# Sample attention with page products in bursts of 16 per four pages, six page buffers, and steps with small array tiles set next to each other

## The chip, the core and the metric

One core of a Trainium2 chip runs the whole program. The metric is the device time of one execution, in microseconds (us). The engines are TensorE (PE), VectorE (DVE), ScalarE (ACT), GpSimd (POOL) and SyncE (SP), which here issues most DMA loads. PE's array has 128 rows and 128 columns; a product may use a part of it, such as 128 rows by 32 columns, and up to four of those lie side by side.

## The reference

One decoder layer for a prompt (512 tokens and 16 meta tokens) and for 8 samples of 8 new tokens, each with 2,048 cached tokens in pages of 128. Differential attention and gated DeltaNet read the same normalised input; their outputs are gated, merged and projected, and a gated ConvFFN follows. The part that the change touches most is the attention of the samples over their cached pages:

```python
k_past = cache_k[l][page_table].reshape(ds, -1, DA_HEADS, 2, DA_HEAD_DIM)
v_past = cache_v[l][page_table].reshape(ds, -1, DA_HEADS, 2 * DA_HEAD_DIM)
...
s_past = jnp.einsum('bqhmd,bkhmd->bhmqk', qs, k_past, preferred_element_type=jnp.float32)
...
pr = jax.nn.softmax(jnp.concatenate([s_past, s_new], axis=-1), axis=-1)
a = pr[:, :, 0] - lam * pr[:, :, 1]
out = (jnp.einsum('bhqk,bkhe->bqhe', a[..., :n_past], v_past.astype(jnp.float32))
       + jnp.einsum('bhqk,bkhe->bqhe', a[..., n_past:], v.astype(jnp.float32)))
```

## The kernel before

The program is written as streams of steps (Python generators). `merge` runs several streams and picks, each time, the stream that has done the smallest share of its planned work (`e[2]` over its weight). A step ends with `yield`, and a number after it is the time, in estimated PE work, for which the stream stays back before its next step, so that ACT and DVE can finish what the next step needs. The numbers come from `DELAY`, or from `PAUSES`, a table that overrides them by stream and by the number of the step. So the order of the instructions of every engine is fixed when the program is built: the merge writes them in an order, and a scheduler then sets the final order by priority and readiness.

Two streams run side by side for the first half of the time: `main` (attention of the prompt, then DeltaNet for four heads, with `gdn_chain`, `gdn_base` and `gdn_solve`) and `rest` (attention of the samples, then the gates and a branch's projection). Behind them come the merge of the branches, the output projection and the ConvFFN, which the change leaves as they are.

`sample_attention` takes two samples at a time (`pr`, four pairs). Its first half goes over four groups `g` of four key pages per sample. For each half group `u` and each sample `e`, `pages` loads two pages (one tile "page", 128x2x512, from a pool of five), PE transposes them (8 transpositions to PSUM "ps_t", of which there are three banks), and ACT or DVE copies them to "KT" (four buffers). Then, after a pause, 8 products of "KT" with "qb" go to "ps_s". Each product uses 128 rows by 32 columns of the array, and the four heads lie side by side. The second half, after the softmax, transposes the probabilities "S" to "pT" and multiplies them with the value pages: 8 products per two tiles "page", again in 32 columns per head.

Loads go through SP's queue in the order of the program; each page load waits until its buffer is free. Products of the DeltaNet's solve use 32x32, 64x64 and other parts of the array; products with weights and the transpositions use the whole.

`qT` (the prompt's queries), `on` (a head's DeltaNet output) and `z2` (its gate) have tiles of their own.

Of the kernel before, what the change touches and what calls it, by code (L numbers as in the profile page):

```python
# [18 lines left out]
SEQ = 512  # L19
# [5 lines left out]
NPG = PAST // PAGE  # L25
H = 4
# [25 lines left out]
def _lay_out_constants():  # L52
# [67 lines left out]
    for name, a in (("c0", c0), ("c1", c1), ("m0", m0), ("m1", m1)):  # L120
# [26 lines left out]
PAUSES = {  # L147
    "gdn_chain0": {
        0: 4.0, 2: 0.87, 3: 0.3, 8: 26.28, 9: 0.49, 10: 0.23, 11: 1.4, 12: 1.21, 13: 0.66, 15: 0.56, 16: 2.98,
        18: 0.39, 19: 0.44, 20: 0.45, 21: 0.63, 22: 0.08, 23: 0.99, 25: 0.74, 26: 0.8, 27: 0.26, 29: 0.85, 33:  # L150
        2.26,
    },
    "gdn_chain1": {
        0: 2.24, 5: 0.96, 8: 25.17, 9: 0.12, 10: 0.89, 11: 0.11, 12: 0.47, 13: 0.57, 15: 1.02, 16: 1.35, 17:
        0.57, 18: 0.28, 19: 1.05, 20: 1.89, 21: 0.59, 24: 0.63, 25: 0.85, 26: 0.37, 27: 0.04, 28: 0.71, 29:
        0.97,
    },
    "gdn_chain2": {
        3: 0.29, 4: 4.82, 7: 0.13, 8: 22.2, 9: 0.02, 10: 0.98, 11: 0.13, 13: 0.08, 15: 1.9, 16: 3.25, 17: 1.24,
        18: 0.74, 19: 1.65, 20: 0.36, 21: 0.38, 22: 0.42, 23: 1.46, 24: 0.23, 25: 0.93, 26: 1.03, 28: 0.54, 29:  # L160
        1.38, 31: 0.02, 33: 0.13,
    },
    "gdn_chain3": {
        8: 19.96, 9: 1.4, 10: 0.21, 11: 1.16, 13: 0.09, 15: 1.11, 16: 2.38, 18: 0.15, 23: 0.5, 25: 0.43, 27:
        0.24, 28: 0.37, 29: 0.39, 30: 0.33,
    },
    "gdn_project0": {
        0: 0.27, 4: 0.32, 6: 4.89,
    },
    "gdn_project1": {  # L170
        2: 0.06, 3: 1.09, 4: 0.1, 6: 35.55,
    },
    "gdn_project2": {
        0: 0.13,
    },
    "main0": {
        6: 0.56, 7: 0.4, 28: 0.8, 42: 0.04, 52: 0.15, 77: 0, 83: 0.89, 86: 0.7, 125: 1.29, 177: 0.4, 192: 0.33,
        201: 0.01, 204: 1.43, 225: 0.46, 241: 1.39, 246: 1.63,
    },
    "make0": {  # L180
        5: 0.99, 6: 0.28, 13: 0.34, 16: 0.4,
    },
    "prompt_rows0": {
        1: 1.38, 3: 7.07, 4: 1.29,
    },
    "prompt_rows2": {
        0: 6.67, 1: 1.83, 4: 0.63,
    },
    "prompt_rows3": {
        2: 0.01, 3: 3.3, 4: 1.66,  # L190
    },
    "prompt_rows4": {
        1: 0.98, 3: 2.79, 4: 1.53,
    },
    "prompt_rows5": {
        2: 0.05, 4: 0.75,
    },
    "prompt_rows6": {
        3: 2.54, 4: 0.64,
    },  # L200
    "prompt_rows7": {
        1: 1.31,
    },
# [7 lines left out]
    },  # L211
    "use0": {
        0: 0.07, 12: 1.51, 13: 0.06, 25: 3.34, 38: 2.47, 39: 0.02, 51: 1.68,
    },
}
# [12 lines left out]
FINE = 8  # L228
MAIN_1 = 582.0
MAIN_2 = 1e9  # L230
REST_W = 163.1

# [2196 lines left out]
```

## Time and profile before

| | |
|---|---|
| median of 3 runs | 1120.28 us (1118.43 to 1120.84) |
| profiled execution, its own time | 1120.4 us |
| its span, first to last instruction | 1118.5 us |
| PE busy / weight loads busy | 1095.2 us / 957.6 us |
| DVE, ACT, POOL busy | 727.8, 520.9, 221.1 us |
| DMA | 156.88 MB, 140 GB/s in the mean |
| granted PE clock | 0.997 |
| key page products (ps_s<-KT,qb) | 512 records, 37.9 us busy |
| value page products (ps_s<-page,pT) | 512 records, 34.4 us busy |

A float32 product with weights that are not float32r stands in the profile as two records, so 16 records are a burst of 8 products. A row of the timeline merges records of the same kind that follow each other; its first number is the start of the first, its second the time to the end of the last, and the xN their count. Since ends overlap, the distance from one row's start to the next row's is what a row costs. Busy times of groups are unions, so four products side by side are not counted four times.

### The profile page before, as it was taken

Reading aid. Unit: us, or ns where it says so; the run is one execution under the profiler, and the core shown is the slowest. Engines: PE = TensorE matmul, PEld = TensorE weight load, DVE = VectorE, ACT = ScalarE, POOL = GpSimd, SP = SyncE. Lnnn points to the kernel's source line nnn. Section 1 sums busy time; section 2 is a strip of 40 time slices with the busy share of each in tenths; the row PEclk is TensorE's granted clock in tenths of the full one; section 3 lists DMA queues with packets and bytes.
Section 4 is the critical chain, followed back from the end, with each engine's and each line's share of the span. In section 5 each row is a group of like instructions: output and inputs, shape, how many; then the busy total and the mean of one; then the engine's idle time right before and its main releaser. Section 6 shows DMA issues by size and latency. Waiting matters only on the chain.

```text
span 1118.5 us, 23304 instructions
## 1 busy us (share of the span) xinstructions
PE 1095.2 (98%) x8554; PEld 957.6 (86%) x8554; DVE 727.8 (65%) x1893; ACT 520.9 (47%) x1256; POOL 221.1 (20%) x340
## 2 busy tenths in 40 slices
PE   9999999999999999999999999999999999999997
PEld 8887787777686697699999987999999999988886
DVE  6455665777486387385345665599999999852315
ACT  6244454555456266352433344465555555832311
POOL 3122220121110100100000004334445454200000
PEclk9999999999999999999999999999999999999999
DMA  7377325747847857833334254423333232333213
GB/s 201 74 247 225 91 71 191 229 131 238 275 149 249 295 153 238 279 83 76 77 79 141 86 162 143 119 67 88 103 87 104 86 106 76 116 113 104 86 47 123
DMA packets 167356, 156.88 MB, mean 140 GB/s; under 512 B 12307, under 2 KB 123458, under 8 KB 167241
## 3 DMA queue, kind: packets, MB, share of 16 engines
q1 hardware_dynamic: 162833, 147.00, 43.1%
q0 software_dynamic: 3008, 5.16, 1.5%
q10 hardware_dynamic: 1400, 3.22, 0.9%
q8 instruction: 68, 1.11, 0.4%
q14 instruction: 47, 0.39, 0.1%
HBM read 145.45 MB, written 9.88 MB: 139 GB/s over the span
## 4 chain that ended last, share of the span: by engine, by line
PE 85%; DMA 4%; ACT 4%; DVE 3%; issue 1%; POOL 1%; SPq 0%; DVEq 0%; ACTq 0%; POOLq 0%
PE ps_d L357 33%; PE ps_t L357 21%; PE ps_g L357 15%; PE ps_s L357 8%; PE ps_t L512 7%; DMA page<-in_cache_v 1%; ACT KT L1566 1%; PE ps_m L357 1%; DMA wraw<-in_w_out 1%; DMA x<-in_x_prompt 1%; DMA page<-in_cache_k 1%; DMA wraw<-in_w_in 1%; ACT whi L406 1%; DVE wlo L407 1%; POOL grr L476 1%
## 5 line engine op out<-in xcount | busy, mean ns | idle before, releaser
L407 DVE TENSOR_TENSOR wlo<-wraw,whi 128x512 fp32r<-128x512 f32 x190 | 143.5, 772 | 109.9 <-ACT whi L406 108.7
L357 PE MATMUL ps_d<-xhi,whi 128*128 128x256 f32 (+2 forms) x696 | 214.2, 311 | 0.1
L357 PE MATMUL ps_d<-xhi,wlo 128*128 128x256 f32 (+2 forms) x696 | 208.7, 303 | 0.0
L357 PE MATMUL ps_d<-xlo,whi 128*128 128x256 f32 (+2 forms) x696 | 208.3, 302 | 0.0
L406 ACT CAST whi<-wraw 128x512 fp32r<-128x512 f32 x190 | 114.0, 620 | 170.1 <-PE ps_d L357 67.6
L357 PEld LDWEIGHTS ps_d<-xhi,whi 128*128 128x128 f32 x696 | 131.8, 191 | 6.5 <-issue 4.3
L357 PEld LDWEIGHTS ps_d<-xlo,whi 128*128 128x128 f32 x696 | 131.5, 190 | 3.6 <-issue 3.2
L357 PEld LDWEIGHTS ps_d<-xhi,wlo 128*128 128x128 f32 x696 | 131.0, 190 | 2.6 <-issue 2.2
L407 DVE TENSOR_TENSOR lw<-sw,hw 128x512 fp32r<-128x512 f32 x76 | 68.7, 904 | 5.2 <-ACT hw L406 5.2
L1566 ACT COPY KT<-ps_t 128x512 f32<-128x512 f32 x106 | 56.7, 596 | 28.4 <-PE ps_t L512 27.9
L512 PE MATMUL ps_t<-consts,page 128*128 128x128 f32 x512 | 67.7, 278 | 1.4 <-DMA page<-in_cache_k 0.6
L357 PE MATMUL ps_t<-fhit,hw 128*128 128x290 f32 x228 | 67.9, 298 | 1.1 <-ACT p L2018 0.6
L512 PEld LDWEIGHTS ps_t<-consts,page 128*128 128x128 f32 x512 | 55.4, 140 | 14.4 <-issue 8.2
L357 PE MATMUL ps_t<-flot,hw 128*128 128x290 f32 x228 | 67.5, 296 | 0.0
L357 PE MATMUL ps_t<-fhit,lw 128*128 128x290 f32 x228 | 67.5, 296 | 0.0
L406 ACT CAST hw<-sw 128x512 fp32r<-128x512 f32 x76 | 46.9, 619 | 15.5 <-PE ps_g L357 9.9
L357 PEld LDWEIGHTS ps_t<-fhit,hw 128*128 128x128 f32 x228 | 43.0, 189 | 1.6 <-ACT p L2018 0.9
L2069 ACT ACTIVATE fy<-fpre,fw 128x592 f32<-128x592 f32 x22 | 19.5, 884 | 51.7 <-DVE fpre L2029 51.7
L357 PEld LDWEIGHTS ps_t<-flot,hw 128*128 128x128 f32 x228 | 43.2, 189 | 0.0
L357 PEld LDWEIGHTS ps_t<-fhit,lw 128*128 128x128 f32 x228 | 43.0, 189 | 0.0
L357 PE MATMUL ps_s<-KT,qb 128*32 128x256 f32 x512 | 37.9, 386 | 0.6
L357 PE MATMUL ps_s<-page,pT 128*32 128x256 f32 x512 | 34.4, 384 | 3.2 <-DMA page<-in_cache_v 3.2
(720 smaller groups left out, 2814.3 us busy)
## 6 DMA issues: line engine op xcount, KB each, us to landing
page<-in_cache_k SPq DMA_DIRECT2D x128, 256.0 KB, 4.3
page<-in_cache_v SPq DMA_DIRECT2D x128, 256.0 KB, 4.4
wraw<-in_w_in SPq DMA_DIRECT2D x86, 256.0 KB, 3.1
wraw<-in_w_ffn_in SPq DMA_DIRECT2D x50, 256.0 KB, 3.1
wraw<-in_w_down SPq DMA_DIRECT2D x44, 256.0 KB, 2.8
raw<-in_w_ffn_in SPq DMA_DIRECT2D x38, 256.0 KB, 2.9
wraw<-in_w_out SPq DMA_DIRECT2D x16, 256.0 KB, 3.1
x<-in_x_prompt SPq DMA_DIRECT2D x4, 512.0 KB, 6.8
```

What stands on the lines that cost most here:

```text
L357: return self.nc.tensor.matmul(out, lhsT, rhs, **kw).ins
L406: self.nc.scalar.copy(hi, raw)
L407: (eng or self.nc.vector).tensor_tensor(out=lo, in0=raw, in1=hi.bitcast(F32), op=ALU.subtract)
L476: nc.gpsimd.tensor_tensor(out=dst, in0=dst, in1=self.mhalf[:rows, :n], op=ALU.pow)
L512: self.nc.tensor.transpose(out, in_, self.ident[:k, :k])
L1566: copy(kt[:, :, 128 * j : 128 * j + 128], tp)
L2069: nc.scalar.activation(y, pre[:, 0:592], AF.Identity, bias=fw[:, m, 19:20], scale=fw[:, m, 16:17])
```

## The change

There are five parts.

1. In `sample_attention` the key products of both half groups are written behind the transpositions of all four tiles: 16 products in one burst per group instead of 8 twice. The value products likewise: four tiles are loaded, then 16 products. The pause between the two bursts of a value group is gone.
2. The page pool has six buffers (`PAGES`) instead of five.
3. Three tiles are no longer made: `on` uses `vn`, `z2` uses `self.ob[:, h]`, `qT` uses `self.oa`.
4. `mm` and `transpose` note whether the last product was small (`narrow`: at most 64 rows, or at most 32 columns). After a small product, `merge` first tries the streams whose next step is marked as small (`Narrow`, `Held`), and a step marked `Held` stays back up to 3.0 longer unless the last product was a small one. The first small product behind a wide one is kept in the program's order by the scheduler.
5. `PAUSES` is a new table, and three weights of the streams are new (`MAKE_W`, `MAIN_1`, `REST_W`).

```diff
-MAKE_W = 65.20437
+PAGES = 6
+MAKE_W = 54.400005891
...
-MAIN_1 = 582.0
+MAIN_1 = 564.54
+HOLD = 3.0
+PAUSES = {
+    "gdn_chain0": {
+        0: 1.49, 2: 0.41, 3: 0.46, 4: 8.2, 6: 0.03, 8: 26.44, 9: 0.34, 10: 0.77, 11: 1.4, 12: 1.21, 13: 1.01,
...
-REST_W = 163.1
+REST_W = 162.95320999999998
+class Narrow(float):
+    hold = 0.0
+class Held(Narrow):
+    hold = HOLD
...
     def mm(self, out, lhsT, rhs, **kw):
...
-        return self.nc.tensor.matmul(out, lhsT, rhs, **kw).ins
+        was, self.narrow = self.narrow, lhsT.shape[0] <= 64 or lhsT.shape[1] <= 32
+        i = self.nc.tensor.matmul(out, lhsT, rhs, **kw)
+        return (self.tc.keep_in_program_order(i) if self.narrow and not was else i).ins
...
     def merge(self, *streams):
-        live = [[g, total, 0.0, 0.0, *self.pauses(g)] for g, total in streams]
+        live = [[g, total, 0.0, 0.0, self.pauses(g), 0, None] for g, total in streams]
         while live:
-            for s in sorted(live, key=lambda e: e[2] / (e[1]() if callable(e[1]) else e[1])):
-                if s[3] > self.work + self.idle + 1e-6:
+            now = self.work + self.idle + 1e-6
+            for s in sorted(live, key=lambda e: (
+                not (self.narrow and e[6] is not None), e[2] / (e[1]() if callable(e[1]) else e[1])
+            )):
+                if s[3] > now or s[6] is not None and not self.narrow and s[3] + s[6] > now:
                     continue
...
-                    s[3] = self.work + self.idle + s[4].get(s[5], delay)
+                    s[3] = self.work + self.idle + s[4].get(s[5], float(delay))
                     s[5] += 1
+                    s[6] = getattr(delay, "hold", None)
...
-        on = self.t(pool, [128, 5, 128], "on")
+        on = vn
...
-        yield DELAY[h][7]
+        yield Narrow(DELAY[h][7])
...
-        z2 = self.t(pool, [128, NQ], "z2")
+        z2 = self.ob[:, h]
...
-        self.qT = self.t(pool, [128, H, SEQ], "qT")
+        self.qT = self.oa
...
-            t = self.t(pool, [128, 2, 512], "page", bufs=5)
+            t = self.t(pool, [128, 2, 512], "page", bufs=PAGES)
...
-                        kts.append(kt)
-                    yield DELAY[pr][26]
-                    for e, kt in reversed(list(enumerate(kts))):
+                        kts[u, e] = kt
+                    yield Held(DELAY[pr][26]) if u else 0.0
+                for u in (1, 0):
+                    for e in (1, 0):
                         for h in range(H):
...
-                yield DELAY[pr][28]
-                for j0 in (0, 2):
-                    vps = [pages(cv, [(2 * pr + e) * NPG + 4 * g + j for e in range(2)]) for j in (j0, j0 + 1)]
-                    for k in (1, 0):
+                yield Held(DELAY[pr][28])
+                vps = [pages(cv, [(2 * pr + e) * NPG + 4 * g + j for e in range(2)]) for j in range(4)]
+                for k in (3, 2, 1, 0):
...
-                    yield DELAY[pr][31]
+                yield DELAY[pr][31]
```

What this does to the order is best seen on PE. Here x4 is a count of instructions (products or transpositions), and the numbers behind names tell the buffers of one name apart.

First place: key pages of the last pair of samples, where little else stands between. Before, a burst of two rows (8 products) follows every two tiles:

```order
L357 MATMUL ps_s_6315<-KT_6393,qb_357 32x256 x4
L357 MATMUL ps_s_6315<-KT_6377,qb_357 32x256 x4
L512 MATMUL ps_t_6435<-consts_66,page_6416 128x128 x2
L512 MATMUL ps_t_6454<-consts_66,page_6441 128x128 x4
L512 MATMUL ps_t_6460<-consts_66,page_6441 128x128 x4
L512 MATMUL ps_t_6478<-consts_66,page_6474 128x128 x4
L512 MATMUL ps_t_6484<-consts_66,page_6474 128x128 x2
L357 MATMUL ps_s_6415<-KT_6453,qb_357 32x256 x4
L357 MATMUL ps_s_6415<-KT_6428,qb_357 32x256 x4
L512 MATMUL ps_t_6484<-consts_66,page_6474 128x128 x2
```

Now, on the same engine at the same place, four rows (16 products) follow four tiles:

```order
L541 MATMUL ps_t_6456<-consts_66,page_6443 128x128 x4
L541 MATMUL ps_t_6462<-consts_66,page_6443 128x128 x4
L541 MATMUL ps_t_6472<-consts_66,page_6468 128x128 x4
L541 MATMUL ps_t_6478<-consts_66,page_6468 128x128 x4
L541 MATMUL ps_t_6488<-consts_66,page_6484 128x128 x4
L541 MATMUL ps_t_6494<-consts_66,page_6484 128x128 x4
L541 MATMUL ps_t_6531<-consts_66,page_6518 128x128 x4
L541 MATMUL ps_t_6537<-consts_66,page_6518 128x128 x2
L381 MATMUL ps_s_6417<-KT_6487,qb_356 32x256 x4
L381 MATMUL ps_s_6417<-KT_6471,qb_356 32x256 x4
L381 MATMUL ps_s_6417<-KT_6455,qb_356 32x256 x4
L381 MATMUL ps_s_6417<-KT_6430,qb_356 32x256 x4
```

What moved: the two bursts of a group stand together, and the transpositions of the next group's first tile stand ahead of the burst.

Second place: value pages of the third pair, beside the DeltaNet's chain (ps_g) and a projection (ps_d). Before, on PE, a burst takes two tiles:

```order
L357 MATMUL ps_s_5401<-page_5609,pT_5569 32x256 x4
L357 MATMUL ps_s_5401<-page_5588,pT_5569 32x256 x4
L357 MATMUL ps_g_5638<-grhs_5622,y_4895 128x128
L357 MATMUL ps_d_5751<-xhi_9_87,wlo_5718 128x322
L357 MATMUL ps_d_5751<-xhi_9_87,whi_5717 128x322
L357 MATMUL ps_d_5751<-xlo_10_88,whi_5717 128x322
L357 MATMUL ps_g_5681<-gv_5640,kn_4559 128x128
```

Now it takes four, and the next burst stands 21 rows behind:

```order
L381 MATMUL ps_s_5275<-page_5602,pT_5552 32x256 x4
L381 MATMUL ps_s_5275<-page_5599,pT_5552 32x256 x4
L381 MATMUL ps_s_5275<-page_5596,pT_5552 32x256 x4
L381 MATMUL ps_s_5275<-page_5575,pT_5552 32x256 x4
L381 MATMUL ps_g_5621<-gv_5573,kn_4788 128x128
L381 MATMUL ps_g_5625<-gS_5560,er_4761 128x128
L381 MATMUL ps_g_5625<-gv_5573,dbig_up_4780 128x128
L381 MATMUL ps_d_5890<-xlo_10_88,whi_5801 128x336
```

What moved: the work that stood between two half bursts stands behind the whole one.

Third place: the solve of the last head (32x32 products from "cc", "dd") beside the last keys. Before, PE has weight products between the small ones:

```order
L357 MATMUL ps_g_6645<-cc_6308,lm_6642 32x32 x16
L357 MATMUL ps_d_7099<-xlo_8_86,whi_7092 128x256
L357 MATMUL ps_d_7099<-xhi_7_85,wlo_7093 128x256
L357 MATMUL ps_s_6515<-KT_6601,qb_357 32x256 x4
L357 MATMUL ps_s_6515<-KT_6585,qb_357 32x256 x4
L357 MATMUL ps_g_6663<-dd_6644,row_6306 32x32 x16
```

Now the small ones of both streams follow each other:

```order
L381 MATMUL ps_s_6517<-KT_6608,qb_356 32x256
L381 MATMUL ps_g_6571<-cc_6302,lm_6568 32x32 x16
L381 MATMUL ps_s_6517<-KT_6608,qb_356 32x256 x3
L381 MATMUL ps_s_6517<-KT_6592,qb_356 32x256
L381 MATMUL ps_g_6621<-dd_6570,row_6300 32x32 x16
L381 MATMUL ps_s_6517<-KT_6592,qb_356 32x256 x3
L381 MATMUL ps_s_6517<-KT_6555,qb_356 32x256
L381 MATMUL ps_g_6641<-cc_6302,dbig_low_5950 32x32 x8
```

What moved: the weight products left the stretch, and the key burst is cut into pieces by the solve's steps, in part within the four products of one tile.

More of the change, by code (lines that the diff above doesn't have):

```diff
@@ L240, in __init__ @@
         self.work = self.idle = 0.0
-        self.made = {}
+        self.made, self.narrow, self.step = {}, False, None
     def name(self, s):
@@ L367, in pauses @@
         self.made[n] = self.made.get(n, -1) + 1
[L368 removed]
+        return PAUSES.get(f"{n}{self.made[n]}", {})
     def merge(self, *streams):
[L374 removed]
+        live = [[g, total, 0.0, 0.0, self.pauses(g), 0, None] for g, total in streams]
         while live:
[L376 to L377 removed]
+            now = self.work + self.idle + 1e-6
[3 more added lines that the diff above has]
+                if s[3] > now or s[6] is not None and not self.narrow and s[3] + s[6] > now:
                     continue
                 before = self.work
+                self.step = s
                 try:
@@ L511, in transpose @@
         self.work += 0.11
-        self.nc.tensor.transpose(out, in_, self.ident[:k, :k])
+        was, self.narrow = self.narrow, k <= 64 or in_.shape[1] <= 32
+        i = self.nc.tensor.transpose(out, in_, self.ident[:k, :k])
+        return (self.tc.keep_in_program_order(i) if self.narrow and not was else i).ins
     def embed(self, pool):
@@ L1098, in gdn_chain @@
             )
-            yield DELAY[h][9]
+            yield Narrow(DELAY[h][9]) if i == 1 else DELAY[h][9]
             if i == 1:
```

144 lines of the change are left out of this document (64 added, 80 removed), and 39 rows, old and new, of the table PAUSES.

## The prediction

> **What bounds the kernel now.** I read the page's busy times and its chain first, then the stretch in which the change lies, then who TensorE (PE) waited for there.
>
> ```profile
> PE 1095.2 (98%) x8554; PEld 957.6 (86%) x8554; DVE 727.8 (65%) x1893; ACT 520.9 (47%) x1256; POOL 221.1 (20%) x340
> PE 85%; DMA 4%; ACT 4%; DVE 3%; issue 1%; POOL 1%; SPq 0%; DVEq 0%; ACTq 0%; POOLq 0%
> 60.00:475.00 415.00, 402.78 (x3838) 314.21 (x3837) 267.32 (x958) 207.61 (x578) 65.03 (x127) 1.00 0.64 204
> PE ps_s L357 <- DMA page<-in_cache_v: 3.2, 4, 1.8
> PE ps_t L512 <- DVE kn L1005: 2.3, 2, 1.4
> PE ps_t L512 <- DVE on L1511: 2.0, 2, 1.0
> ```
>
> PE is busy for 98% of the span and is 85% of the chain. In the third row, the stretch from the first page transposition to the last value page (60 to 475 us), PE is busy for 402.8 of 415 us at a granted clock of 1.00, so only 12.2 us of idle time can be won or lost by waits as they are. The next three rows are the longest of those waits. So the change is worth what it takes from, or adds to, PE's busy time, plus the new idle time. "Busy" hides something, though: the distance from one product's start to the next differs with its neighbours. That is where the change works.
>
> ```profile
> 258.32 0.66 PE L512 MATMUL ps_t<-consts,page 128*128 128x128 f32 x4
> 258.90 1.07 PE L357 MATMUL ps_s<-KT,qb 128*32 128x256 f32 x16
> 259.91 2.26 PE L512 MATMUL ps_t<-consts,page 128*128 128x128 f32 x18
> 272.58 1.93 PE L357 MATMUL ps_s<-page,pT 128*32 128x256 f32 x32
> 274.45 0.45 PE L357 MATMUL ps_g<-cc,lm 32*32 32x32 f32 x32
> 274.83 0.65 PE L512 MATMUL ps_t<-consts,S 128*128 128x128 f32 x4
> 275.42 0.45 PE L357 MATMUL ps_g<-dd,row 32*32 32x32 f32 x32
> 276.92 1.07 PE L357 MATMUL ps_s<-page,pT 128*32 128x256 f32 x16
> 277.92 0.44 PE L357 MATMUL ps_g<-dd,row 32*32 32x32 f32 x16
> 406.28 0.66 PE L512 MATMUL ps_t<-consts,page 128*128 128x128 f32 x4
> 406.69 0.36 PE L357 MATMUL ps_d<-xlo,whi 128*128 128x256 f32 x1
> 406.89 1.51 PE L512 MATMUL ps_t<-consts,page 128*128 128x128 f32 x12
> 408.16 0.37 PE L357 MATMUL ps_d<-xhi,wlo 128*128 128x256 f32 x1
> ```
>
> The first column is the start; "128*32" is the part of the array that a product uses (rows by columns), and an f32 product of pages stands as two records, so 16 records are 8 products. One burst of 16 holds PE from 258.90 to 259.91, 1.01 us. A burst of 32 holds it from 272.58 to 274.45, 1.87 us. So 16 more records cost 0.86 us and the burst itself has a fixed part of 0.15 us. The wide neighbours pay too: four transpositions between two small shapes take 274.83 to 275.42, 0.59 us, while twelve in an undisturbed row take 406.89 to 408.16, 0.106 us each, 0.42 for four. That is 0.17 more. The weight products (float32r) show the same:
>
> ```profile
> 266.31 0.39 PE L357 MATMUL ps_d<-xhi,whi 128*128 128x256 f32 x1
> 266.53 0.28 PE L357 MATMUL ps_d<-xlo,whi 128*128 128x256 f32 x1
> 266.65 0.28 PE L357 MATMUL ps_d<-xhi,wlo 128*128 128x256 f32 x1
> 267.25 0.27 PE L357 MATMUL ps_d<-xlo,whi 128*128 128x256 f32 x1
> 267.46 0.43 PE L357 MATMUL ps_s<-kTs,qb 128*32 128x64 f32 x16
> ```
>
> They start 0.12 us apart (266.53 to 266.65), but 0.22 after the first one behind a small burst and 0.21 before the next: 0.10 and 0.09 more. So one visit to a small shape from the full array costs 0.15 + 0.17 = 0.32 us, or 0.15 + 0.19 = 0.34, beyond its work; I take 0.30, since the neighbour's part is shared where a visit is followed by another.
>
> **The change part by part.** *Bursts and neighbours.* Counted through PE's whole order, the array is left for a smaller shape and entered again 129 times before and 85 times now: 44 visits fewer, 13.2 us at 0.30. The work is the same 7,400 products. Changes from one small shape straight to another rise from 24 to 42. Their price is in 276.92 to 277.92: a burst of 16 between two small groups still holds PE for 1.00 us, 0.14 over the 0.86 of its work; I take 0.15, so 18 cost 2.7 us. In two of the four heads the steps now cut groups of four column tiles in two (place three in the part on the change, rows with a product alone and then x3); each cut sends one pass more, about a quarter of 0.86, 0.2 us, and there are 14 against 8 before: 1.2 us. Net -9.3, with bounds of -6 (visits at 0.22, cuts doubled) and -14 (visits at 0.34, small-to-small at 0.1).
>
> *Key copies.* Before, each burst of 8 key products stands close behind the transpositions that feed it:
>
> ```profile
> 336.29 1.07 PE L357 MATMUL ps_s<-KT,qb 128*32 128x256 f32 x16
> 337.29 2.04 PE L512 MATMUL ps_t<-consts,page 128*128 128x128 f32 x16
> 339.38 1.07 PE L357 MATMUL ps_s<-KT,qb 128*32 128x256 f32 x16
> L1566 ACT COPY KT<-ps_t 128x512 f32<-128x512 f32 x106 | 56.7, 596 | 28.4 <-PE ps_t L512 27.9
> ```
>
> Sixteen transpositions take 337.29 to 339.38, 2.09 us, where 16 x 0.106 + 0.17 gives 1.87: some 0.1 to 0.2 us is the wait for the last copy to KT (0.596 us). With half as many bursts, about 12 of these go: -1.4 us. On the other side stands that KT still has four buffers and one burst now uses all four, so copies of the next group wait for this group's products. In the row, PE's own pace is 4 x 0.106 = 0.42 us a tile and ACT's copy 0.6 us or a little less when piped, so over the eight tiles of a group ACT falls up to 1.4 us behind, of which three PSUM banks take up most. I put both together at -0.5, between -2 and +5.
>
> *Transpositions among weight products.* Runs of either kind become shorter: changes between them rise by about 60, 30 visits. 406.28 to 408.16 holds such a visit: 16 transpositions and one product in 1.88 us, against 16 x 0.106 + 0.12 = 1.82. At up to 0.04 each, +0.5 (0 to +1.2).
>
> *Value pages.* A burst now needs four tiles (two pages each) of six buffers at once; before it needed two of five. All four loads stand on SP's queue in the order they are used by, so the first product of a burst waits for the youngest load.
>
> ```profile
> page<-in_cache_v SPq DMA_DIRECT2D x128, 256.0 KB, 4.4
> DMA to landing us min/median/max: 2.7/4.3/5.8
> 370.00:398.00 28.00, 26.96 (x241) 21.19 (x241) 11.79 (x33) 7.46 (x23) 3.01 (x4) 1.00 0.94 322
> 371.07 1.07 PE L357 MATMUL ps_s<-page,pT 128*32 128x256 f32 x16
> 378.05 1.07 PE L357 MATMUL ps_s<-page,pT 128*32 128x256 f32 x16 [0.48 <-DMA page<-in_cache_v]
> ```
>
> A load takes 4.4 us to land, 5.8 at worst, with the DMA engines 94% busy in such a stretch. The burst at 378.05 waited 0.48 us for pages whose buffers the burst of 371.07 to 372.07 had given back: from give-back to use some 6.2 us are needed there. I added up, with the spacings above, the PE work that stands in the new order between the product that frees a buffer and the product that needs its next page: 4.7, 5.3, 5.6 and 6.0 us at the four shortest of the twelve later bursts, the rest 6.3 and more; before, the shortest was 5.9. Against 6.2 that is 1.5 + 0.9 + 0.6 + 0.2 = 3.2 us. The two spare tiles are fetched during the burst before, so nothing else is exposed. The 3.2 us of the old waits may stay or go. I take +3, between -2 (the old ones go, landing is at its 2.7 minimum) and +10 (all twelve wait 0.8). While PE waits for a page, the whole queue behind it waits.
>
> *Shorter chains in the DeltaNet solve.* With small steps set next to each other, a product stands nearer to the copy it needs: 46 waits with under 0.8 us of PE work from producer to user, against 28, short by 3 us more in all. Where before had them, little came of it: of all waits of the chain's products ("ps_g") the list for 60 to 475 us has this one.
>
> ```profile
> PE ps_g L357 <- DVE st L1088: 0.3, 1, 0.3
> ```
>
> So +1.5, between 0 and +5.
>
> *In-place tiles* ("on" in "vn", "z2" in "ob", "qT" in "oa"). Each is written where its last reader has run in the same chain (scores of a head before its output, the right-hand side before its product), so they cost nothing; the cover is that very order. After the last value burst the rest of PE's order is the same up to a few rows. SP's queue holds the same loads in order, and a page load behind a weight load waits with it for that load's buffer:
>
> ```profile
> SPq L402 <- DVE wlo L407: 157.4, 55, 15.1
> ```
>
> In the third pair of samples four weight loads now stand ahead of the last group's youngest pages. DVE has then split the older weights long before, as far as the order shows, so this stands at 0, and its worst, one wait of up to 15 us of which PE would feel a part, is inside the +10.
>
> Sum: -9.3 - 0.5 + 0.5 + 3 + 1.5 = -4.8; and of the 12.2 us of idle time in the stretch, the waits for DVE quoted at the top (2.3 + 2.0 us, places where nothing else stood ready) meet another order; I count half as gone, -2. That is -6.8 against the profiled execution's own 1120.4 us (span 1118.5 and 1.9 around it), which is 0.1 over the median of the runs: **1113.6 us**.
>
> **A rule to weigh.** The rows price a change of shape at about 0.15 us (0.30 a visit, in and out). The Trainium skill, "TensorEngine Tiling (Array Packing)", section "Key Properties", says that changing the tiling mode drains TensorE, and "TensorE: Matmul & The Clock Gate", "Step-by-step: what each phase is for", gives the drain as about 128 cycles, which at 2.4 GHz would be an estimate of 53 ns. By that figure 70 changes fewer would give 3.7 us where the rows give about 10, and the whole sum would come to about 1119. The trace agrees that there is a stop at each change; its size is nearer to three drains, and I go by the rows.
>
> **The rivals.** *Pages become the bound (slower).* Place: the value bursts. If a burst can only start when four loads after the last burst have landed, then the cycle is a burst of 1.87 us and then 4.4 to 5.8 us to landing, 6.3 to 7.7, and 2 MB per group at 322 GB/s alone is 6.5. Where the order leaves 6.3 to 7 us between bursts, each of twelve would wait about 1, and the key groups, with the same six buffers, 0.3 each: 12 + 5 = 17 against a saving of 9.3: 1125 to 1128. It decides from a mean wait of 0.8 us per value burst on. For it speaks the 94% in the row; against it, that the mean in the whole stretch is 64% and that two tiles are always ahead. *The saving is given back in the chains (same).* KT's four buffers are one group's, so ACT's 0.6 a copy sets the pace in the stretches with nothing but pages: 16 groups x 0.4 to 0.6 us more, 6 to 10 in all: 1118 to 1122. Against it: PE has other work between most groups. *Only the drain counts (same).* The price per visit is 0.1, not 0.3: -4.4, and with the waits -0.5: about 1120. Against it stand two kinds of neighbours in the rows with the same 0.3. The skill's drain, above, would end here too. *More is saved.* The idle time before DVE goes as a whole and visits cost 0.34: -14 - 4 + 1: 1103 to 1106.
>
> **How the numbers follow.** My forecast (1107 to 1118) 0.62; more saved 0.15; pages the bound 0.09; given back 0.10; only the drain 0.04. A run of this kernel can be told from no change from about 0.2% on, 2.2 us. Faster than 1118.0: 0.62 + 0.15 + 0.01 = 0.78; within: most of the two middle cases and a start of the page case, 0.12; slower than 1122.5: 0.10. The range reaches to 1104 and to 1121, leaving about 0.06 below and 0.13 above.
>
> **What the new profile would show.** Right: page and key bursts of 32 records that hold PE about 1.87 us; PE's busy time down by some 8 to 11 us in the stretch to 475 us, the weight stages behind it unchanged and earlier; the wait for in_cache_v at 3 to 6 us in all. Wrong: a row of waits for in_cache_v of 1 us each before nearly every burst, or for KT's copy before the key bursts; or PE busy time down by less than 5 us, if a change of shape is cheaper than I read; or a new wait of some us for DVE or POOL in the DeltaNet chain, whose steps are now held for one another.

## The result, and the profile after

The changed kernel takes 1110.39 us (median of 4 runs, 1107.89 to 1111.44) against 1120.12 us for the kernel before (4 runs on the same chip, 1118.43 to 1120.84). The ratio is 0.9912, with a 95% interval of 0.9891 to 0.9933: 9.7 us less. The forecast was 1113.6 us, 6.7 us less. The profiled execution took 1109.7 us, with a span of 1107.9 us and a granted clock of 0.998.

The page of the changed kernel, busy times and shares of the chain:

```profile
PE 1082.5 (98%) x8554; PEld 958.0 (86%) x8554; DVE 726.1 (66%) x1891; ACT 521.2 (47%) x1258; POOL 220.4 (20%) x340
PE 80%; DVE 8%; ACT 4%; DMA 3%; issue 3%; POOL 2%; SPq 0%; DVEq 0%; ACTq 0%; POOLq 0%
```

PE has the same 8554 records as before and is busy for 12.7 us less (1095.2 to 1082.5). The span is 10.6 us shorter. So the gain is PE's own time with the same work, and some 2 us of it went into idle time. About 1 us of the 12.7 is no matter of the change: in this one execution of the kernel before, the granted clock of the first 60 us was 0.97, in that of the changed kernel 1.00. The stretch from 60 to 475 us, and then the list of waits in it (total, times, longest):

```profile
60.00:475.00 415.00, 401.90 (x3916) 326.33 (x3915) 276.34 (x978) 215.05 (x601) 63.94 (x127) 1.00 0.65 207
```

```profile
PE ps_s L381 <- DMA page<-in_cache_v: 1.7, 2, 1.3
PE ps_g L381 <- DVE cc L1225: 1.6, 2, 1.0
PE ps_g L381 <- DVE st L1118: 1.4, 2, 0.7
PE ps_s L381 <- ACT KT L1596: 1.2, 1, 1.2
PE ps_t L541 <- DVE on L1541: 1.2, 1, 1.2
PE ps_t L541 <- DVE KT L1596: 1.1, 2, 0.5
PE ps_t L541 <- ACT KT L1596: 0.8, 1, 0.8
...
PE ps_t L541 <- DVE kn L1036: 0.3, 1, 0.3
```

In this stretch PE handles 3916 records where it handled 3838 before, in about the same busy time: 78 records of the work behind have moved up. The idle part is 13.1 us (415 less 401.90) against 12.2. The waits are other ones than before: the value pages fell from 3.2 to 1.7 us, kn from 2.3 to 0.3, on from 2.0 to 1.2, while the DeltaNet solve (ps_g behind cc and st) rose from 0.3 to 3.0 us and the copies to KT show 1.2 before one key burst and 1.9 before transpositions, where 0.6 stood in all.

The timeline of PE at the last key pages, and three later value bursts of the same view (the second number of a row runs to the end of its last record):

```profile
413.48 1.93 PE L381 MATMUL ps_s<-KT,qb 128*32 128x256 f32 x32
415.34 4.22 PE L541 MATMUL ps_t<-consts,page 128*128 128x128 f32 x34
419.61 1.93 PE L381 MATMUL ps_s<-KT,qb 128*32 128x256 f32 x32
421.48 3.24 PE L541 MATMUL ps_t<-consts,page 128*128 128x128 f32 x26
...
438.29 1.93 PE L381 MATMUL ps_s<-page,pT 128*32 128x256 f32 x32
...
445.38 1.93 PE L381 MATMUL ps_s<-page,pT 128*32 128x256 f32 x32
...
451.68 1.93 PE L381 MATMUL ps_s<-page,pT 128*32 128x256 f32 x32
```

A burst of 32 records holds PE for 1.86 us (413.48 to 415.34), as forecast. The value bursts start 7.1 and 6.3 us apart and show no idle time before them (the view shows it from 0.15 us on). A key burst with the transpositions up to the next one takes 6.13 us (413.48 to 419.61); these are 34, two more than belong to a group, so a group alone takes some 5.92 (less 2 x 0.106). Two half groups took 6.18 before (2 x 3.09, from 336.29 to 339.38). So in these rows the merged burst saves about 0.26 us even where there is nothing but key pages.

### The profile page after: what moved, and what is told of

Read it like the earlier page. It is cut to its first block, busy times and chain, and to the rows that moved or that the text cites. A ratio compares the mean times of both kernels' runs of the same rounds, so it can differ in the third digit from the quotient of the medians.

```text
span 1107.9 us, 23301 instructions
## 1 busy us (share of the span) xinstructions
PE 1082.5 (98%) x8554; PEld 958.0 (86%) x8554; DVE 726.1 (66%) x1891; ACT 521.2 (47%) x1258; POOL 220.4 (20%) x340
## 4 chain that ended last, share of the span: by engine, by line
PE 80%; DVE 8%; ACT 4%; DMA 3%; issue 3%; POOL 2%; SPq 0%; DVEq 0%; ACTq 0%; POOLq 0%
PE ps_d L381 30%; PE ps_t L381 21%; PE ps_g L381 15%; PE ps_s L381 6%; PE ps_t L541 6%; ACT KT L1596 1%; PE ps_m L381 1%; DMA wraw<-in_w_out 1%; DVE wlo L435 1%; DVE cy L880 1%; DMA x<-in_x_prompt 1%; DMA page<-in_cache_v 1%; DVE xc L1217 1%; DVE row L1215 1%; DVE row L1216 1%
## 5 line engine op out<-in xcount | busy, mean ns | idle before, releaser
L381 PE MATMUL ps_t<-fhit,hw 128*128 128x290 f32 x228 | 67.9, 298 | 0.5 <-DVE p L2124 0.5
L434 ACT CAST hw<-sw 128x512 fp32r<-128x512 f32 x76 | 46.8, 618 | 15.7 <-PE ps_g L381 10.5
L2101 DVE SCALAR_TENSOR_TENSOR fy<-fpre,fw,fy 128x592 f32<-128x592 f32 x44 | 36.4, 828 | 1.0 <-ACT fy L2099 0.4
L381 PE MATMUL ps_s<-KT,qb 128*32 128x256 f32 x512 | 34.1, 383 | 1.5 <-ACT KT L1596 1.2
```

The source lines that it names most:

```text
L381: i = self.nc.tensor.matmul(out, lhsT, rhs, **kw)
L434: self.nc.scalar.copy(hi, raw)
L2101: nc.vector.scalar_tensor_tensor(out=y, in0=pre[:, j : j + 592], scalar=fw[:, m, 16 + j : 17 + j], in1=y, op0=ALU.mult, op1=ALU.add)
```

## The experiments

All times below are medians of runs on one core, each beside runs of the kernel before on the same chip (1120.1 to 1121.0 in the four comparisons). "More" or "less" is against 1110.39 us unless said otherwise. The four medians of the kernel before differ by 0.9 us, so differences under 1 us say nothing. A visit is, as in the prediction, leaving the full array for a smaller shape and coming back; counts of visits are taken from PE's whole order, where a product with more than 64 rows and more than 64 columns counts as full. The theory (A) is that the gain is 44 visits fewer at a fixed price, less some waits. The rivals are that the sixth buffer brought it, or that changes of shape are cheap and the new order and its table of pauses brought it.

**What a visit costs, measured by itself.** Three kernels put something small between float32r products in the ConvFFN, far behind the changed part, at 57 places. The first adds one 32x32 product (two records), the second a product of the whole array with the same 32 columns, the third a 128x32 product and then the 32x32 one.

```diff
 def product(ps, wt, x, first):
     ...
+    if first:   # first kernel
+        self.nc.tensor.matmul(ps[0:32, 0:32], self.ident[0:32, 0:32], self.ident[0:32, 0:32], start=True, stop=True)
+    if first:   # second kernel
+        self.nc.tensor.matmul(ps[0:128, 0:32], self.ident, self.ident[:, 0:32], start=True, stop=True)
+    if first:   # third kernel
+        self.nc.tensor.matmul(ps[0:32, 0:32], self.ident[:, 0:32], self.ident[:, 0:32], start=True, stop=True)
+        self.nc.tensor.matmul(ps[0:32, 0:32], self.ident[0:32, 0:32], self.ident[0:32, 0:32], start=True, stop=True)
```

> The changed kernel with one extra 32x32 product (two records) ahead of 57 products of the ConvFFN, into PSUM space that the next product overwrites. Nothing waits for it, and the merge of the streams ends long before. Theory A (each visit to a small shape costs PE about 0.3 to 0.37 us beyond its work, in and out together): 57 x 0.35 = 20 us more than the changed kernel, about 1130 us. Rival B (a change of shape only drains the array, 0.05 us each way): 57 x 0.1 and the product's own 0.03 give 7 us more, about 1118. Rival C (the gain of the change came from its order and waits, and a visit costs next to nothing): within 3 us of 1110.

> The same 57 extra products at the same places, but over the whole array (128 rows, 128 columns, 32 moving columns), so without a change of shape. All theories: only the extra work, 57 x 0.05 to 0.1 = 3 to 6 us more than the changed kernel, 1113 to 1117. If it costs as much as the run with small products, it is the extra product and not its shape that costs, and A falls.

> Two extra products at each of the 57 places: one of 128 rows by 32 columns, then one of 32x32, so each visit holds a change from small to small too. Theory A with 0.15 to 0.18 us for that change: 57 x 0.17 = 10 us more than the run with one small product, about 1140. Rival B: 57 x 0.08 = 5 more, about 1123. Rival C: still near 1110 to 1113.

Measured: 1131.54 us (1131.16 to 1131.73, ratio 1.0100 [1.0081, 1.0118]) for the 32x32 product, 21.1 more, so 0.37 us for each; 1123.0 (1121.5 to 1124.44, ratio 1.0025 [1.0015, 1.0035]) for the full-array product, 12.6 more, 0.22 each; 1141.03 (1140.71 to 1142.04, ratio 1.0185 [1.0166, 1.0203]) for the two shapes, 9.5 over the first kernel, 0.17 each. The first and the third came out as A expected. The second cost 12.6 us where every theory had 3 to 6, so part of what the first kernel pays is not the price of the shape. One place in the timeline of each of the three, in this order:

```profile
839.45 0.29 PE L381 MATMUL ps_g<-flo,hw 128*128 128x290 f32 x1
839.59 0.29 PE L381 MATMUL ps_g<-fhi,lw 128*128 128x290 f32 x1
839.81 0.24 PE L2041 MATMUL ps_t<-consts 32*32 32x32 f32 x2
839.98 0.40 PE L381 MATMUL ps_t<-fhi,whi 128*128 128x290 f32 x1
840.22 0.30 PE L381 MATMUL ps_t<-flo,whi 128*128 128x290 f32 x1
```

```profile
837.01 0.30 PE L2041 MATMUL ps_t<-consts 128*128 128x32 f32 x2
837.15 0.38 PE L381 MATMUL ps_t<-fhi,whi 128*128 128x290 f32 x1
837.37 0.30 PE L381 MATMUL ps_t<-flo,whi 128*128 128x290 f32 x1
```

```profile
837.09 0.30 PE L381 MATMUL ps_g<-fhit,lw 128*128 128x290 f32 x1
837.32 0.25 PE L2041 MATMUL ps_d<-consts 128*32 128x32 f32 x2
837.50 0.24 PE L2042 MATMUL ps_d<-consts 32*32 32x32 f32 x2
837.67 0.40 PE L381 MATMUL ps_d<-fhi,whi 128*128 128x290 f32 x1
837.91 0.30 PE L381 MATMUL ps_d<-flo,whi 128*128 128x290 f32 x1
```

Undisturbed products start 0.135 us apart. In the first fence the last product before the visit takes 0.22 us (839.59 to 839.81), the small product 0.17, and the first product behind it 0.24: 0.63 in place of 0.27, so 0.36. In the second the product itself takes 0.14 and the first one behind it 0.22, 0.085 more than undisturbed: here this part of a visit's price also stands behind a float32 product (not float32r) of the whole array. The shape then adds 0.36 - 0.22 = 0.14, with the two products' own work set equal. In the third fence each extra shape takes 0.17 to 0.18, its product's own work included.

The weight loads (PEld) show where the shape's part lies. The first four rows are of the first kernel, the last one of the second:

```profile
839.46 0.19 PEld L381 LDWEIGHTS ps_g<-fhi,lw 128*128 128x128 f32 x1
839.80 0.13 PEld L2041 LDWEIGHTS ps_t<-consts 32*32 32x32 f32 x2 [0.16 <-PE ps_g L381]
839.98 0.19 PEld L381 LDWEIGHTS ps_t<-fhi,whi 128*128 128x128 f32 x1
840.09 0.19 PEld L381 LDWEIGHTS ps_t<-flo,whi 128*128 128x128 f32 x1
...
836.88 0.32 PEld L2041 LDWEIGHTS ps_t<-consts 128*128 128x128 f32 x2
```

The weights of the product at 839.59 are loaded from 839.46 on, beside the product before it. Those of the small product start at 839.80, together with the product itself (839.81), and so do those of the wide one behind it (839.98). The full-array product at 837.01 has its weights loaded from 836.88 on. So in these rows the weights are not loaded ahead at a change of shape. How much of the price is this load and how much a stop of another kind, no run separates.

**The same price inside the bursts.** One full-array transposition (of the identity) goes into the middle of each of the 32 page bursts; for comparison the same 32 transpositions stand among the others that precede the bursts.

```diff
                 for u in (1, 0):
+                    if u == 0:
+                        self.nc.tensor.transpose(sp[:, 0:128], self.ident, self.ident)
+                        self.narrow = False
                     for e in (1, 0):
...
                 for k in (3, 2, 1, 0):
+                    if k == 1:
+                        self.nc.tensor.matmul(acc[:, 256:384], self.ident, self.ident, is_transpose=True, start=False, stop=False)
+                        self.narrow = False
```

```diff
                             tp = self.ps4("t")
+                            if u == e == j == 0:
+                                self.nc.tensor.transpose(tp[:, 0], self.ident, self.ident)
                             for h in range(H):
...
+                self.nc.tensor.transpose(tp[:, 0], self.ident, self.ident)
                 for j in range(4):
                     self.transpose(tp[:, j], S[:, 512 * g + 128 * j : 512 * g + 128 * j + 128])
```

> The kernel after with one full-array transposition (128x128, of the identity) set into the middle of each of the 32 bursts of 16 page products; the rest of PE's order is the same. Visits to a small shape rise from 85 to 115. Theory A (a visit costs 0.36 us wherever it stands): 30 x 0.36 + 32 x 0.106 for the transpositions themselves = 14.2 us, so 1124.6 us (1122 to 1128). Rival B (visits cost little; the gain came from the new table's order): only the transpositions' own time, 3.4 to 5 us, so 1114 to 1115.5.

> The kernel after with the same 32 transpositions, but each set among other transpositions, ahead of the first one of a group, so that PE is not taken from one shape to another by them: 87 visits, 36 changes from one small shape to another. Theory A: 32 x 0.106 + 2 x 0.36 - 6 x 0.17 = 3.1 us, so 1113.5 us. Rival B: the same 3 us. The difference to the kernel with the same transpositions in the bursts is the price of the cut alone: A says about 11 us, B 0 to 2.

Measured: 1124.73 us (1122.79 to 1126.94, ratio 1.0042 [1.0027, 1.0057]) and 1113.53 us (1111.01 to 1114.78, ratio 0.9931 [0.9917, 0.9946]). Both are A's numbers within 0.2 us, closer than the runs can tell (their intervals are some 1.6 us to either side), and rival B (cheap changes) is out. The difference, 11.2 us, lies between kernels with the same instructions and 115 against 87 visits. Six more changes from one small shape to another take 1.0 of it; the rest is 0.36 for each of 28 visits, or 0.32 for each of the 32 cuts, with some 0.08 to either side by the two intervals. A cut burst in the timeline of the first:

```profile
413.71 1.07 PE L381 MATMUL ps_s<-KT,qb 128*32 128x256 f32 x16
414.71 0.33 PE L1601 MATMUL ps_s<-consts 128*128 128x128 f32 x1
414.97 1.07 PE L381 MATMUL ps_s<-KT,qb 128*32 128x256 f32 x16
415.97 0.37 PE L381 MATMUL ps_g<-kk 128*80 128x80 f32 x2
```

The burst holds PE from 413.71 to 415.97, 2.26 us, where the whole one took 1.86 and a transposition takes 0.106: 0.29 for the cut. So in this row, with a transposition as its wide neighbour, a visit costs a little less than the 0.36 between float32r products, and near the 0.26 that a merged key group showed.

**The page buffers.** The changed kernel with five buffers, and the kernel before with six (and the three in-place tiles, which make the room).

```diff
-PAGES = 6
+PAGES = 5
```

```diff
-            t = self.t(pool, [128, 2, 512], "page", bufs=5)
+            t = self.t(pool, [128, 2, 512], "page", bufs=6)
...
-        on = self.t(pool, [128, 5, 128], "on")
+        on = vn
```

> The changed kernel with the page pool back at five buffers. Theory A (the gain comes from fewer changes of shape; PE has 87 visits here against 85): the page waits grow by what the missing buffer exposes. If pages are ahead enough, within 2 us of 1110; if the sixth buffer is what makes bursts of four tiles possible, the twelve later value bursts wait 0.5 to 1 us each, 1116 to 1122. Rival D (the gain comes from the sixth buffer): all of it goes, 1120.

> The kernel before with only two parts of the change: the in-place tiles and six page buffers; bursts of 8, the old table and the old merge. 126 visits to small shapes, as before (129). Theory A (the gain is the visits; the sixth buffer only keeps four-tile bursts from waiting, which cost 8 us with five): no gain, since the old waits for pages are 3.8 us in all: 0 to -3, 1117 to 1121. Theory D (the sixth buffer gives the gain by itself): -8, near 1112.

Measured: 1118.47 us (1117.21 to 1122.64, ratio 0.9986 [0.9972, 0.9999]) with five; 1121.14 us (1119.78 to 1123.88, ratio 1.0006 [0.9995, 1.0017]) for the kernel before with six. So the sixth buffer and the in-place tiles bring nothing by themselves, and bursts of 16 without it keep 1.6 of their 9.7 us. The waits for pages in the list of the five-buffer kernel, 60 to 475 us:

```profile
PE ps_s L381 <- DMA page<-in_cache_v: 3.4, 3, 1.3
PE ps_t L541 <- DMA page<-in_cache_k: 1.7, 2, 1.2
```

PE waits 1.7 us more for value pages, and 1.7 for key pages, for which the changed kernel's list has no row. Other waits grew too, for DVE: kn to 1.8, ob to 1.4, oS to 1.3 us. PE's idle time grows from 18.0 to 25.1 us over the whole span, at 87 visits. So some 3.4 of these 7.1 us are waits for pages themselves; the rest are waits for other things, in an order that shifted by the missing buffer and with a table of pauses made for six. How much of that rest each of the two accounts for is not shown.

**The order of the merge.** Five kernels. The first takes away the preference for small steps (and the hold, and the kept program order); the second cuts each burst of 16 at a step of its own, so that other streams can come between; the third keeps every small product in the program's order, not only the first of a row. All three keep the new table of pauses, though it was made for another order. The fourth is the changed kernel without a table, the fifth the kernel before without one.

```diff
...
-            for s in sorted(live, key=lambda e: (
-                not (self.narrow and e[6] is not None), e[2] / (e[1]() if callable(e[1]) else e[1])
-            )):
+            for s in sorted(live, key=lambda e: e[2] / (e[1]() if callable(e[1]) else e[1])):
...
```

```diff
...
                 for u in (1, 0):
+                    if u == 0:
+                        yield Cut(1.5)
                     for e in (1, 0):
...
                 for k in (3, 2, 1, 0):
+                    if k == 1:
+                        yield Cut(1.5)
```

```diff
-        return (self.tc.keep_in_program_order(i) if self.narrow and not was else i).ins
+        return (self.tc.keep_in_program_order(i) if self.narrow else i).ins
```

```diff
-PAUSES = {
...
+PAUSES = {}
```

> The changed kernel with the merge of before: no small-first choice, no hold, nothing kept in program order at a small product. 113 visits against 85, small-to-small changes 17 against 42. Theory A, with 0.36 a visit and 0.17 from small to small: 28 x 0.36 - 25 x 0.17 = 5.8 us more than the changed kernel, about 1116, and the waits of an order that the table was not made for on top, 0 to 6. Theory E (bursts alone hold the gain, the small-first order only adds waits): 1108 to 1111.

> The changed kernel with each burst of 16, of keys and of values, cut into 8 and 8 by a step at which other streams may put their work between. 108 visits, 30 small-to-small changes. Theory A: 23 x 0.36 - 12 x 0.17 = 6.2 us more than the changed kernel, about 1117, give or take 4 for the waits of a shifted order. Theory F (the gain is in the order and the new table, the length of the bursts is nothing): within 2 us of 1110.

> The changed kernel with every small product kept in program order by the scheduler, not the first of a burst alone, so that a burst is not cut by another stream's small steps: 87 visits, 24 small-to-small changes against 42. Theory A: 2 x 0.36 - 18 x 0.17 = 2.3 us less than the changed kernel, and 14 cut groups fewer at 0.2, 2 to 3 us less: 1105 to 1108. Against it: a product that may not be passed keeps its readiness as a wait, so if the scheduler's freedom was worth more, 1111 to 1116.

> The kernel after with an empty PAUSES, so that every pause is the one written in DELAY: 93 visits and 27 changes between small shapes, against 121 and 34 in the kernel before with an empty table. Theory A (the bursts bring the gain, the table only places them): 28 x 0.36 + 7 x 0.17 = 11.3 us less than the kernel before without its table, waits apart; both some 10 to 25 us above their own tuned versions because of waits. Rival B (the new table brings the gain): the two without tables are equal within 3 us, or this one is slower.

> The kernel before with an empty PAUSES: 121 visits, 34 changes between small shapes. Some 10 to 25 us slower than before, from waits that the table had removed (1130 to 1145). Theory A: some 11 us above the kernel after with an empty table, waits apart. Rival B: within 3 us of it, or below it.

Measured: 1141.6 us (ratio 1.0185 [1.0171, 1.0199]) without the preference; 1139.56 us (1.0178 [1.0160, 1.0196]) with cut bursts; 1124.79 us (1.0044 [1.0030, 1.0057]) with all small products in program order; 1127.03 us (1.0060 [1.0038, 1.0081]) for the changed kernel without a table; 1119.99 us (0.9989 [0.9977, 1.0001]) for the kernel before without one. A's expectations missed in all five. The first three are 17 to 20 us slower than the upper ends of A's ranges (1122, 1121 and 1108). Without tables the changed kernel is 7 us slower than the kernel before, although it has 28 visits fewer: the sign that rival B gave, but not for its reason, since visits had their price in the experiments above. The old table is worth nothing that can be measured, the new one 16.6 us. So "the bursts bring the gain" is only half of it: they take the visits away, and the new table keeps PE from having to wait for that. That the table alone brought the gain is out all the same: with it, PE's idle time is 2.2 us more than in the kernel before (18.0 against 15.8, the account below), and the gain is in PE's busy time.

The waits show where. For the changed kernel without its table, the costliest wait, then the clock in pieces of 5 us (the number behind the five engines is the granted clock; DMA share and GB/s follow), then the timeline:

```profile
PE ps_t L460 <- DVE kn L954: 5.1, 2, 4.7
```

```profile
475.00:480.00 5.00, 1.04 (x11) 0.72 (x7) 2.73 (x9) 1.39 (x7) 2.44 (x2) 0.75 0.63 159
480.00:485.00 5.00, 3.46 (x15) 2.88 (x16) 3.29 (x15) 2.08 (x6) 0.10 (x1) 0.50 0.02 3
485.00:490.00 5.00, 5.00 (x34) 5.00 (x33) 4.10 (x7) 1.05 (x2) 0.00 (x0) 0.72 0.00 0
490.00:495.00 5.00, 5.00 (x38) 5.00 (x38) 4.39 (x22) 1.92 (x5) 0.00 (x0) 1.00 0.00 0
```

```profile
480.76 0.36 PE L460 MATMUL ps_t<-consts,kn 80*128 80x80 f32 x1 [4.72 <-DVE kn L954]
...
483.79 2.08 PE L300 MATMUL ps_g<-kk 128*128 128x128 f32 x8 [0.46 <-ACT kk L966]
485.66 1.91 PE L300 MATMUL ps_g<-q,kk 128*128 128x128 f32 x8
```

Within and behind one wait of 4.72 us for DVE, which ends at 480.76, the granted clock is 0.75, 0.50 and 0.72 in three pieces of 5 us, and 1.00 from the fourth on. The eight records of kk take 1.87 us (483.79 to 485.66). The same group in the kernel with a transposition in each burst took 0.93 (416.32 to 417.25) at full clock:

```profile
416.32 1.10 PE L381 MATMUL ps_g<-kk 128*128 128x128 f32 x8
417.25 1.77 PE L541 MATMUL ps_t<-consts,page 128*128 128x128 f32 x14
```

So the long wait is paid for twice. In the kernel with stepwise cut bursts it is worse (waits of 4.8 us for value pages up to 488.91 and 3.5 for cc up to 496.08): its clock is 0.50 from 490 to 500 us.

```profile
490.00:495.00 5.00, 2.55 (x24) 0.89 (x16) 4.29 (x26) 1.55 (x3) 0.00 (x0) 0.50 0.03 8
495.00:500.00 5.00, 1.29 (x36) 0.73 (x36) 3.43 (x9) 1.06 (x5) 0.00 (x0) 0.50 0.42 108
```

And the third, with all small products in program order, waits for value pages 6 times:

```profile
PE ps_s L381 <- DMA page<-in_cache_v: 10.2, 6, 5.5
```

**One account for all of them.** With the prices measured above (0.36 us a visit, 0.17 a change between small shapes), PE's idle time from the records of one profiled execution each, and an estimate of the time lost to a lower clock (1 less the mean granted clock, times PE's busy time, to about 1 us), every kernel can be set against the changed one:

| kernel | visits | small to small | by price | idle, more | clock, more | sum | measured |
|---|---|---|---|---|---|---|---|
| changed | 85 | 42 | | (18.0) | (2.2) | | 1110.4 |
| before | 129 | 24 | +12.8 | -2.2 | +1.1 | +11.7 | +9.7 |
| before, six buffers | 126 | 28 | +12.4 | -1.6 | -1.1 | +9.7 | +10.8 |
| before, no table | 121 | 34 | +11.6 | -2.8 | +2.2 | +11.0 | +9.6 |
| five buffers | 87 | 37 | -0.1 | +7.1 | +1.1 | +8.1 | +8.1 |
| all in program order | 87 | 24 | -2.3 | +13.0 | +4.3 | +15.0 | +14.4 |
| no table | 93 | 27 | +0.3 | +10.5 | +4.3 | +15.1 | +16.6 |
| no small-first | 113 | 17 | +5.8 | +17.4 | +8.8 | +32.0 | +31.2 |
| cut at a step | 108 | 30 | +6.2 | +14.8 | +9.9 | +30.9 | +29.2 |

The sums meet the measurements within 2 us, so no further cause of that size is needed. The idle time is taken as it was measured; the sums do not say what caused it. What stays open is whether the three other orders, each with a table made for it, would lose these waits, and whether the one with stepwise cut bursts would then be slower by its 23 visits alone (8 us): no such table was tried.

## Why the prediction was right, by its own steps

The time lies inside the 1107 to 1118 that the prediction gave its own forecast; the gain is 9.7 us, not 6.7. The mechanism held, and the difference lies mostly in the first step.

**The saving on visits: right in kind, too small.** The prediction took 44 visits at 0.30 for 13.2 us. The two sums over all records, with the steady pace of each kind taken off, are about 48.2 us for 129 visits before and 30.9 for 85 after: some 17.3 us, 0.37 and 0.36 each. The isolated kernel gave 0.37, its small product's own work included. The step that failed is the sentence "I take 0.30, since the neighbour's part is shared where a visit is followed by another": in the mean over all visits it is not. The rows themselves had been read well: in the first isolated kernel the neighbours pay 0.085 and 0.105, the 0.19 of the prediction, and the small product takes 0.17, where it had 0.15. Without the discount its 0.34 a visit would have given 15.0 us. The bounds of -6 and -14 for the whole step do not come out of the prices named for them: visits at 0.22 and cuts doubled give -4.6 (9.7 less 2.7 and 2.4), visits at 0.34 and 0.1 from small to small -12.0 (15.0 less 1.8 and 1.2). By the records the step is about -13.0 (17.3 less 3.0 and 1.3), which lies inside the bounds as written and outside them as worked out.

**Changes between small shapes and cut groups: right.** Forecast 2.7 and 1.2 us; the records give about 3.0 (24 to 42 changes) and 1.3, and the isolated kernel 0.17 a change, its product included, against 0.15 taken.

**Waits: the sum was right, the parts were not.** The prediction had +3 for value pages, +1.5 for the solve's chains, -2 for waits for DVE, -0.5 for key copies and +0.5 for mixed transpositions, +2.5 together. The idle time of all records rose from 15.8 to 18.0 us, by 2.2. That these agree is luck, since errors of either sign cancelled. The value pages fell by 1.5 us. The four waits of 1.5, 0.9, 0.6 and 0.2 us were worked out with 6.2 us from a buffer's give-back to the use of its next page, a figure from one place; the list has two waits, of 1.3 and 0.4. The 6.2 was too large for the new order: it was read where a burst started 6.98 us behind the one whose buffers it reused (371.07 to 378.05) and still waited, while in the timeline above the bursts of 445.38 and 451.68 start 6.30 us apart and the second shows no wait. The median landing of a value page was 4.0 us, not 4.4; of key and value pages together the median was 4.2 and the longest 7.0, where it had been 5.8. How much of the waits that stayed away is due to the landing is not shown:

```profile
page<-in_cache_v SPq DMA_DIRECT2D x128, 256.0 KB, 4.0
DMA to landing us min/median/max: 2.7/4.2/7.0
```

With the bounds of -2 to +10 the fall of 1.5 us lay inside, and the term of +3 had the wrong sign. The chains of the solve took 2.7 us more instead of 1.5, the waits for DVE (kn, on) 2.8 less instead of 2, and the waits for KT's copies rose by 2.5 us (from 0.6 to 3.1, 1.2 of it in front of a burst), where the prediction took 0.5 off for both sides of that step. The rival that the saving is given back there did not come: a group of key pages alone became 0.26 us shorter, not longer by 0.4 to 0.6.

**The rivals.** "Pages become the bound" did not come with six buffers; with five, PE waits 7.1 us more, of which 1.7 for value pages and 1.7 for key pages. "Only the drain counts" is out: 0.17 a change by itself and 0.36 a visit. The Trainium skill, "TensorEngine Tiling (Array Packing)", section "Key Properties", with the 128 cycles of the Trainium skill's "TensorE: Matmul & The Clock Gate", section "Step-by-step: what each phase is for", gave an estimate of 53 ns a change; the runs show a stop where the shape changes, as the first page says, but some three times as long as the estimate. The 1119 that the prediction names for that figure leaves out its 1.2 for cut groups; with all its terms the sum is 1120.4. "More is saved" (1103 to 1106) was nearer on the visits' price and wrong on the idle time, which did not go.

**The signs named for the new profile.** Bursts of 32 records at 1.87 us: 1.86. PE's busy time down by 8 to 11 us in the stretch to 475 us: the stretch holds 78 more records now, so only the whole span can be compared, 12.7, of which about 1 is the clock of its start and the rest fits the larger price of a visit. The stages behind: the ConvFFN's products ps_t<-fhit,hw are busy for 67.9 us in both kernels. The wait for value pages at 3 to 6 us: 1.7, a miss. Of the signs of being wrong, no row of 1 us waits stands before the bursts, only one of 1.3 before a value burst and one of 1.2 before a key burst. But "a new wait of some us for DVE or POOL in the DeltaNet chain" came in part: 2.7 us more behind cc and st.

## What to carry to other kernels

Count how often PE leaves the full array and comes back; between float32r products each visit cost 0.36 us here (a full-array product in its place still cost 0.22). A merge of two visits saves such a price without touching the work: 0.26 us in the key groups, with transpositions as neighbours. A longer burst needs more tiles at once, so give it the buffers with it: here five buffers in place of six, with the same table of pauses, took back 8.1 of 9.7 us. And do not expect a table of pauses to fit another order: the three orders that kept it though it was made for another had 13 to 17 us more idle time, and by estimate 4 to 10 us more by the clock.

## What the hardware showed that was not expected

- Around a wait of 4.7 us the granted clock fell to 0.75, 0.50 and 0.72 in three pieces of 5 us, while the waits of up to 1.3 us in the changed kernel leave it at 1.00 in the stretch to 475 us. Two more kernels narrow it: without the preference, a wait of 3.83 us (up to 347.54) is followed by 0.60, 0.50 and 0.88 in the pieces from 345 us on, and with all small products in program order, one of 2.59 us (up to 381.00) leaves 1.00 in the pieces from 375 to 390. In the kernels without a fitting table the lower clock costs, by the estimate above, 4 to 10 us on top of the waits. The Trainium skill, "TensorE: Matmul & The Clock Gate", section "Part 1: The HAM clock gate", says that an idle window of about 3.4 us brings the clock back to half; the traces agree with 0.50 behind waits of 3.83 and 4.72 us and 1.00 around one of 2.59.
- A small float32 product of the whole array between float32r products costs 0.22 us, of which 0.085 stands in the first float32r product behind it. So a part of a visit's price is no matter of shape. At a change of shape the weights of the next product start to load only with the product itself, 0.22 us behind the start of the one before it (839.80); without a change they load beside the one before.
- The table of the kernel before was worth nothing that can be measured (0.9989 [0.9977, 1.0001] without it), the new one 16.6 us. Why the new order needs its table so much more is not shown.
